# Where the final norm of the first 384 tokens is multiplied and stored: in one piece behind the last tokens' norm, or a tile per step of the last output products

## The chip, the cores and the metric

The kernel runs on one core of a Trainium2 chip. The metric is the device time of one execution in microseconds (us); lower is better. The engines are named as in the profile: PE (TensorE, with PEld for its weight loads), DVE (VectorE), ACT (ScalarE), POOL (GpSimd) and SP (SyncE, which here only issues DMAs).

## The reference

One inference step of a two-layer backbone (a Mamba-2 mixer, then differential attention, each followed by a gated convolutional feed-forward part), for 128 context tokens and 512 latent tokens of width 1024. Only its end matters here: the second layer's feed-forward part, its gated residual, and the final norm.

```python
def _rms(x):
    xf = x.astype(F32)
    return xf * lax.rsqrt(jnp.mean(xf * xf, axis=-1, keepdims=True) + EPS)

def rmsnorm(x, g):
    return (_rms(x) * g.astype(F32)).astype(x.dtype)
...
        xp = xp + p_g2 * conv_ffn(modulate(xp, norm_ffn_g[i], p_sh2, p_sc2), *ffn_p)
        xs = xs + s_g2 * conv_ffn(modulate(xs, norm_ffn_g[i], s_sh2, s_sc2), *ffn_p)
    y_prompt = rmsnorm(xp, final_norm_g)
    y_sample = rmsnorm(xs, final_norm_g)
```

## The kernel before

All activations are kept transposed: the width of 1024 lies in eight tiles of 128 partitions (`KT = 8`), and the 640 tokens lie along the free dimension. The residual stream is `self.x[0..7]`, which the profile calls `xr`. Matrix products are done three times in halves of a split float32 number (`mh`/`ml` and `whi`/`wlo`), so each step over one block of 128 inputs is three matmuls per part of the tokens.

The last feed-forward part ends in `project_last`, which makes the eight output tiles `po` of the down projection. For the first five tiles all 640 tokens are done at once. The last three tiles are done by parts of the tokens: first part C (tokens 0 to 383) of the three tiles, then part D (tokens 384 to 639) of the three. After each tile and part, `gate_add` on DVE adds the gated product to `xr` (L224; two instructions of 128 tokens for part D, since 128 of its tokens are latent and 128 context), and `norm_sq` squares the result on ACT (`nsq`, `sq`).

When a part's three tiles are written, its final norm is put in the list of tasks (`final_task`). A task is a generator; `hook()` is called after every step over one block of inputs (eight steps for each of the last tiles) and runs every task whose wait is over. `yield n` means: go on n steps later. `final_task` first makes the statistics: 32 small matmuls sum the squares into `ms`, nine small DVE instructions make the reciprocal root `rs_y`, and eight small matmuls spread it over the partitions into the PSUM tile `nbc`. Then, for each of the eight tiles, one DVE instruction makes `yt` = `xr` x gain x `nbc`, and a DMA stores it to `yT`: from the SP queue, for part D every second one from the ACT queue. The slots of `yt` come from a ring of 19 (`NF`) that other tiles also use.

Part C's task runs its statistics beside part D's products. Then it meets `yield 99`, which is more than the steps that are left, so its multiplications and stores come when the leftover tasks are drained, and these are drained in reverse order: part D's first, part C's behind it:

```python
            for t in reversed(list(self.tasks)):
                self.drain(t)
```

The order in which the engines receive the instructions is settled when the program is built; each engine then works through its own list in that order. `self.stt` is the DVE instruction of L224, and `self.mm` the matmul of L230.

Of the kernel before, what the change touches and what calls it, by code (L numbers as in the profile page):

```python
# [167 lines left out]
class Step:  # L168
# [1159 lines left out]
    def final_task(self, half):  # L1328

        bc = yield from self.norm_stats(half)  # L1330
        c0, c1 = HALF[half]
        if half == "C":
            yield 99
        for i in range(KT):
            t = self.slot("f", f"yt{i}", bufs=NF)
            self.stt(t[:, c0:c1], self.x[i][:, c0:c1], self.gains[:, 4 * KT + i:4 * KT + i + 1], bc[:, :c1 - c0],
                     ALU.mult, ALU.mult)
            eng = self.nc.scalar if half == "D" and i % 2 else self.nc.sync
            eng.dma_start(self.a["yT"][i, :, c0:c1], t[:, c0:c1])
# [211 lines left out]
```

## Time and profile before

| | |
|---|---|
| median of 3 runs | 1862.02 us (1861.01 to 1862.44) |
| profiled execution, its own time | 1865.19 us |
| span of the profiled execution, first to last instruction | 1863.4 us |
| PE busy | 1830.9 us, 98% of the span |
| DVE busy | 1464.3 us, 79% |
| ACT busy | 998.1 us, 54% |
| last matmul of part D's products starts | 1846.44 us |
| last multiplication of part C starts | 1859.46 us |
| last store is issued | 1860.10 us |

Times inside the profile count from the start of the span. A row of the timeline gives start, duration, engine, source line, operation, the tile written and those read, and shapes; in brackets stands how long the engine was idle before it and what ended that. The whole change lies in the last 25 us of the span.

### The profile page before, as it was taken

How to read it: one execution, taken by the hardware profiler on the slowest of the kernel's cores; microseconds unless marked ns; L12 is line 12 of the kernel's file. 1: busy time of each engine (PE TensorE's matmuls, PEld its weight loads, DVE VectorE, ACT ScalarE, POOL GpSimd, SP SyncE). 2: the span in 40 equal slices, each digit the busy share in tenths (PEclk: the TensorE clock that was granted, in tenths of full speed). 3: DMA queues.
4: the chain of work that ended last, by engine and by line, in shares of the span. 5: the costliest groups of instructions: out<-in, count | busy, mean ns of one | idle time of the engine just before them, and what ended most of it. 6: DMA issues, size and time to landing. Idle time of an engine off the chain costs nothing.

```text
span 1863.4 us, 33068 instructions
## 1 busy us (share of the span) xinstructions
PE 1830.9 (98%) x13057; PEld 1715.6 (92%) x13057; DVE 1464.3 (79%) x2827; ACT 998.1 (54%) x1862; POOL 55.7 (3%) x84
## 2 busy tenths in 40 slices
PE   7999999999999999999999999999999999999997
PEld 5899999999989999999999988888899999999996
DVE  5689999999848999998586877778779874874874
ACT  3379686879426442244363566566546543643641
POOL 0000000000001100011000000000001011100000
PEclk9999999999999999999999999999999999999998
DMA  9734244445547976677642211111047368853421
GB/s 339 270 108 147 92 126 128 114 132 177 184 148 220 279 217 211 208 205 201 208 133 77 88 46 59 57 52 49 21 129 193 95 180 237 250 166 103 142 80 57
DMA packets 108675, 276.06 MB, mean 148 GB/s; under 512 B 12284, under 2 KB 19048, under 8 KB 102504
## 3 DMA queue, kind: packets, MB, share of 16 engines
q1 hardware_dynamic: 100520, 225.19, 37.4%
q0 software_dynamic: 7424, 48.24, 11.0%
q8 instruction: 102, 1.67, 0.4%
q10 hardware_dynamic: 576, 0.52, 0.1%
q14 instruction: 53, 0.43, 0.1%
HBM read 267.95 MB, written 54.19 MB: 173 GB/s over the span
## 4 chain that ended last, share of the span: by engine, by line
PE 93%; DVE 3%; ACT 2%; DMA 1%; issue 1%; SPq 0%; DVEq 0%; ACTq 0%
PE po L230 25%; PE up L230 14%; PE bb L230 6%; PE ba L230 6%; PE bc L230 6%; PE z L230 6%; PE x L230 5%; PE st L230 5%; PE v L230 3%; PE yp L230 3%; PE q L230 2%; PE sl L230 2%; PE k L230 2%; PE ov L230 2%; PE in L230 1%; PE wt L1275 1%
## 5 line engine op out<-in xcount | busy, mean ns | idle before, releaser
L221 ACT ACTIVATE whi<-raw 128x1024 fp32r<-128x1024 f32 (+4 forms) x266 | 270.9, 1020 | 318.8 <-PE po L230 189.9
L227 DVE TENSOR_TENSOR wlo<-raw,whi 128x1024 fp32r<-128x1024 f32 (+4 forms) x266 | 312.4, 1175 | 79.8 <-ACT whi L221 68.2
L224 DVE SCALAR_TENSOR_TENSOR xr<-po,mod,xr 128x256 f32<-128x256 f32 (+2 forms) x231 | 89.0, 433 | 123.6 <-PE po L230 123.5
L230 PE MATMUL po<-ml,whi 128*128 128x256 f32 (+1 forms) x704 | 168.1, 310 | 0.0
L230 PE MATMUL po<-mh,whi 128*128 128x256 f32 (+1 forms) x704 | 167.8, 310 | 0.0
L230 PE MATMUL po<-mh,wlo 128*128 128x256 f32 (+1 forms) x704 | 167.8, 309 | 0.0
L230 PEld LDWEIGHTS po<-mh,whi 128*128 128x128 f32 x704 | 128.1, 188 | 0.8 <-ACT mh L221 0.5
L230 PEld LDWEIGHTS po<-mh,wlo 128*128 128x128 f32 x704 | 128.7, 188 | 0.0
L230 PEld LDWEIGHTS po<-ml,whi 128*128 128x128 f32 x704 | 128.5, 188 | 0.1
L230 PE MATMUL up<-h01h,wlo 128*128 128x256 f32 x464 | 105.7, 308 | 0.0
L230 PE MATMUL up<-h01l,whi 128*128 128x256 f32 x464 | 105.6, 308 | 0.0
L230 PE MATMUL up<-h01h,whi 128*128 128x256 f32 x464 | 105.6, 308 | 0.0
L230 PEld LDWEIGHTS up<-h01h,whi 128*128 128x128 f32 x464 | 84.4, 188 | 0.0
L230 PEld LDWEIGHTS up<-h01h,wlo 128*128 128x128 f32 x464 | 84.4, 188 | 0.0
L230 PEld LDWEIGHTS up<-h01l,whi 128*128 128x128 f32 x464 | 84.3, 188 | 0.0
L221 ACT ACTIVATE mh<-cv 128x640 fp32r<-128x640 f32 x44 | 32.4, 737 | 88.3 <-DVE cv L227 88.3
L221 ACT ACTIVATE e<-sl,sm 128x640 f32<-128x640 f32 x64 | 50.4, 790 | 40.2 <-DVE sm L1212 39.8
L688 DVE CUSTOM_DVE_ANT_0 junk<-mw,cbc 128x1024 bf16<-128x1024 f32 x48 | 58.5, 1219 | 8.4 <-DMA mw<-in_modT 8.3
L230 PE MATMUL z<-h00h,whi 128*128 128x256 f32 (+1 forms) x256 | 62.9, 325 | 0.0
L221 ACT ACTIVATE ca<-ca 128x640 f32<-128x640 f32 x44 | 32.3, 735 | 55.4 <-DVE ca L224 55.3
L230 PE MATMUL bb<-T,whi 128*128 128x320 f32 x264 | 61.6, 313 | 0.0
L221 ACT ACTIVATE e<-rb,Ctok 128x128 f32<-128x128 f32 x160 | 56.3, 389 | 8.5 <-issue 6.1
(580 smaller groups left out, 5317.5 us busy)
## 6 DMA issues: line engine op xcount, KB each, us to landing
wsum<-in_w_blk POOLq DMA_DIRECT2D x42, 768.0 KB, 7.1
raw<-in_w_blk SPq DMA_DIRECT2D x55, 512.0 KB, 4.0
mw<-in_modT SPq DMA_DIRECT2D x48, 512.0 KB, 4.4
raw<-wsum SPq DMA_DIRECT2D x92, 256.0 KB, 3.0
raw<-in_w_in SPq DMA_DIRECT2D x40, 512.0 KB, 5.4
rb<-rowd SPq DMA_DIRECT2D x40, 512.0 KB, 5.6
raw<-in_w_dn SPq DMA_DIRECT2D x32, 448.0 KB, 3.4
raw<-in_w_qkv SPq DMA_DIRECT2D x24, 512.0 KB, 3.3
```

The lines of the kernel that those rows point to most:

```text
L221: return self.pin(self.nc.scalar.activation(out, in_, func, **k))
L224: return self.pin(self.nc.vector.scalar_tensor_tensor(out, in0, s, in1, op0, op1))
L227: return self.pin(self.nc.vector.tensor_tensor(out, a, b, op))
L230: return self.pin(self.nc.tensor.matmul(out, lhsT, rhs, start=start, stop=stop, **k))
L688: nc.vector.tensor_tensor_reduce(w if c else junk, w, cb[:, c, :], 1.0, 0.0, ALU.mult, ALU.add, self.mod[l][:, t, c:c + 1])
L1275: nc.tensor.transpose(pm[:, b * P:(b + 1) * P], ws[b][:, kc * P:(kc + 1) * P], self.ident)
```

## The change

Part C's task no longer waits 99 steps ahead of its loop. It waits one step ahead of each of its eight tiles, so that a multiplication and a store are handed out with each of eight steps of part D's products. The instructions themselves stay the same, in number, shape and engine.

```diff
         bc = yield from self.norm_stats(half)
         c0, c1 = HALF[half]
-        if half == "C":
-            yield 99
         for i in range(KT):
+            if half == "C":
+                yield 1
             t = self.slot("f", f"yt{i}", bufs=NF)
```

On DVE, at the place where part D's residual additions stand (`xr_5203` and `xr_5205` are the residual tiles 6 and 7; those of 128 columns belong to part D), this is the piece of the difference:

```order
 L224 SCALAR_TENSOR_TENSOR rs_y<-rs_a,rs_y 128x96
+L224 SCALAR_TENSOR_TENSOR yt_20232<-xr_5191,gains,nbc 128x384
+L224 SCALAR_TENSOR_TENSOR yt_20238<-xr_5193,gains,nbc 128x384
+L224 SCALAR_TENSOR_TENSOR yt_20247<-xr_5195,gains,nbc 128x384
+L224 SCALAR_TENSOR_TENSOR yt_20253<-xr_5197,gains,nbc 128x384
+L224 SCALAR_TENSOR_TENSOR yt_20259<-xr_5199,gains,nbc 128x384
+L224 SCALAR_TENSOR_TENSOR yt_20265<-xr_5201,gains,nbc 128x384
+L224 SCALAR_TENSOR_TENSOR yt_20271<-xr_5203,gains,nbc 128x384
+L224 SCALAR_TENSOR_TENSOR yt_20277<-xr_5205,gains,nbc 128x384
 L224 SCALAR_TENSOR_TENSOR xr_5203<-po,mod_104,xr_5203 128x128 x2
 L224 SCALAR_TENSOR_TENSOR xr_5205<-po,mod_104,xr_5205 128x128 x2
```

The eight multiplications of part C now stand in one block behind part C's `rs_y` and ahead of part D's last four residual additions; before, they were the last eight instructions of DVE.

At the end of DVE's list stand part D's eight multiplications. In the kernel after the change they carry these waits (a name with `DMAHW` is the arrival of a DMA of the SP or ACT queue, here of a store that read the slot before):

```order
L224 SCALAR_TENSOR_TENSOR yt_20350<-xr_5191,gains,nbc 128x256 [waits DMAHW4_49,PE_49]
L224 SCALAR_TENSOR_TENSOR yt_20353<-xr_5193,gains,nbc 128x256 [waits DMAHW5_49]
L224 SCALAR_TENSOR_TENSOR yt_20356<-xr_5195,gains,nbc 128x256 [waits DMAHW6_49]
L224 SCALAR_TENSOR_TENSOR yt_20359<-xr_5197,gains,nbc 128x256 [waits DMAHW7_49]
L224 SCALAR_TENSOR_TENSOR yt_20362<-xr_5199,gains,nbc 128x256 [waits Activation_49]
L224 SCALAR_TENSOR_TENSOR yt_20365<-xr_5201,gains,nbc 128x256 [waits DMAHW0_49]
L224 SCALAR_TENSOR_TENSOR yt_20368<-xr_5203,gains,nbc 128x256 [waits DMAHW1_49]
L224 SCALAR_TENSOR_TENSOR yt_20371<-xr_5205,gains,nbc 128x256 [waits Activation_49]
```

Before, the first of these eight waited only for PE (`nbc`) and the other seven for nothing; now six of them are also told to wait for a store of part C, whose slot they take over.

SP's list before ended with four stores of part D (128x256) and the eight of part C (128x384), the last of them in this order:

```order
L1339 DMA out_yT<-yt_20338 128x256
L1339 DMA out_yT<-yt_20344 128x256
L1339 DMA out_yT<-yt_20350 128x384
L1339 DMA out_yT<-yt_20353 128x384
L1339 DMA out_yT<-yt_20356 128x384
L1339 DMA out_yT<-yt_20359 128x384
```

Now the eight of part C come first, and SP ends with four stores of part D:

```order
L1339 DMA out_yT<-yt_20265 128x384
L1339 DMA out_yT<-yt_20271 128x384
L1339 DMA out_yT<-yt_20277 128x384
L1339 DMA out_yT<-yt_20350 128x256
L1339 DMA out_yT<-yt_20356 128x256
L1339 DMA out_yT<-yt_20362 128x256
L1339 DMA out_yT<-yt_20368 128x256
```

ACT's list keeps its four stores of part D at its end. The lists of PE and POOL are the same as before.

## Prediction

> **What bounds the kernel now.** I read the page's summary first, then the chain of work that ended last in its final 20 us, then DVE's timeline there, and then the stores.
>
> ```profile
> span 1863.4 us, 33068 instructions
> ...
> PE 93%; DVE 3%; ACT 2%; DMA 1%; issue 1%; SPq 0%; DVEq 0%; ACTq 0%
> ```
>
> PE carries 93% of the chain, and the change leaves PE's list alone. So only the end, where PE no longer carries the chain, can move:
>
> ```profile
> 1845.90 0.84 PE po L230 x7
> ...
> 1847.40 0.42 ACT sq L221
> ...
> 1847.87 0.36 PE ms L230 x8
> ...
> 1850.67 1.95 PE nbc L230 x8
> ...
> 1857.44 2.62 DVE yt L224 x5
> ```
>
> Columns: start, duration, what. Behind the last product (the matmul rows end at 1846.73) the chain runs through part D's residual addition, square, sum, reciprocal root, the spreading matmuls, and then DVE's `yt` multiplications up to 1860.06. There are sixteen of these, D's eight and then C's eight. C's eight need only part C's `nbc`, which had been ready much earlier (below). They sit on the end path because of their place in DVE's list.
>
> ```profile
> 1836.22 0.62 DVE L224 SCALAR_TENSOR_TENSOR xr<-po,mod,xr 128x384 f32<-128x384 f32 x1 [3.62 <-PE po L230]
> ...
> 1843.93 0.61 DVE L224 SCALAR_TENSOR_TENSOR xr<-po,mod,xr 128x128 f32<-128x128 f32 x2 [2.92 <-PE po L230]
> 1846.76 0.61 DVE L224 SCALAR_TENSOR_TENSOR xr<-po,mod,xr 128x128 f32<-128x128 f32 x2 [2.21 <-PE po L230]
> ...
> 1852.64 7.42 DVE L224 SCALAR_TENSOR_TENSOR yt<-xr,gains,nbc 128x256 f32<-128x256 f32 x16 [2.12 <-PE nbc L230]
> ```
>
> This is DVE alone. The numbers in brackets show the room that the block moves into: DVE idles 2.92 us before the additions of tile 6 and 2.21 us before those of tile 7, waiting for PE's products both times. That is 5.13 us of holes, but tile 6's pair stands between them, and DVE works through its list in order.
>
> **The change part by part.** *What leaves the end.* C's eight multiplications as a group (busy time, mean ns of one), and their pace in the timeline:
>
> ```profile
> L224 DVE SCALAR_TENSOR_TENSOR yt<-xr,gains,nbc 128x384 f32<-128x384 f32 x8 | 4.3, 608 | 0.0
> ```
>
> ```profile
> 1855.78 1.13 DVE L224 SCALAR_TENSOR_TENSOR yt<-xr,gains,nbc 128x384 f32<-128x384 f32 x2
> ...
> 1859.46 0.61 DVE L224 SCALAR_TENSOR_TENSOR yt<-xr,gains,nbc 128x384 f32<-128x384 f32 x1
> ```
>
> The eight of C start at 1855.78 (first) and 1859.46 (eighth): seven steps, 0.526 us each, the next one starting before the last has ended (a single one takes 608 ns). The stores behind them:
>
> ```profile
> 1855.90 0.34 ACTq L1339 DMA_DIRECT2D out_yT<-yt  x1
> ...
> 1860.10 0.33 SPq L1339 DMA_DIRECT2D out_yT<-yt  x1
> ```
>
> ```profile
> out_yT<-yt SPq DMA_DIRECT2D x8, 192.0 KB, 1.9
> out_yT<-yt SPq DMA_DIRECT2D x4, 128.0 KB, 1.8
> out_yT<-yt ACTq DMA_DIRECT2D x4, 128.0 KB, 1.8
> ```
>
> D's last store goes out at 1855.90 (ACT queue, 1.8 us to landing), C's last at 1860.10 (SP queue, 1.9). When C's are no longer behind D's, the last store is issued 4.20 us earlier and lands 0.1 sooner: 4.30 us. The data bear this out from the other side:
>
> ```profile
> 1856.30:1860.20 3.90, 0.00 (x0) 0.00 (x0) 3.77 (x8) 0.00 (x0) 0.00 (x0) 0.50 0.97 349
> ...
> 1861.60:1861.80 0.20, 0.00 (x0) 0.00 (x0) 0.00 (x0) 0.00 (x0) 0.00 (x0) 0.50 0.17 56
> ```
>
> The last two columns are the share of the DMA engines and GB/s. In the last row a share of 0.17 is left, so the data stop near 1861.65, and the span ends at 1863.4, so 1.75 us of ending follows, which I leave as it is. D's eight stores are 1.05 MB; at 349 GB/s they need 3.0 us, about their pace on DVE (C's first starts 1855.78 - 1852.64 = 3.1 us behind D's first), so the DMA engines keep up and do not set a later end of their own.
>
> *What the block costs where it goes.* It waits for C's `nbc`:
>
> ```profile
> 1841.07 1.13 PE L230 MATMUL nbc<-rs_y,cst 128*128 128x96 f32 x8
> ```
>
> ```profile
> 1841.02:1843.93 2.91, 2.91 (x26) 2.87 (x26) 0.00 (x0) 0.28 (x1) 0.00 (x0) 1.00 0.00 0
> 1844.54:1846.76 2.22, 2.22 (x27) 2.09 (x29) 0.01 (x2) 0.42 (x1) 0.00 (x0) 1.00 0.00 0
> ```
>
> ```profile
> L224 DVE SCALAR_TENSOR_TENSOR xr<-po,mod,xr 128x128 f32<-128x128 f32 x2 | 0.6, 346 | 2.9 <-PE po L230 2.9
> ```
>
> `nbc` is done at 1842.20, and DVE starts 0.03 later. Eight at 0.526 fill 1842.23 to 1846.44. All four D additions stand behind them. Tile 6's pair was ready at 1843.93 and is now 2.5 us late, which by itself costs nothing: its square joins a sum that also needs tile 7's. Tile 7's pair was ready at 1846.76. Four additions take three steps and one whole one: a pair of 0.61 us with one at 346 ns makes the step 0.264, so 3 x 0.264 + 0.35 = 1.14 and the last ends at 1847.58, against 1847.37 before. The delay of the chain is **0.21 us**. ACT's square of tile 6 then runs 1847.00 to 1847.42, ahead of the one of tile 7 at 1847.60, so ACT adds nothing; PE's sums of tile 6 take about 0.36 us and also end before those of tile 7 begin.
>
> The step of 0.526 was measured with PE and its PSUM traffic at rest. The nearest row beside running matmuls is the addition of the same shape (128x384, a PSUM operand) at 1836.22: 0.62 us against 0.608, so I keep the step. The bounds: no delay at all (a block 0.21 us shorter), or no overlap between neighbours, 8 x 0.608 = 4.86 plus two pairs of 0.61, which ends at 1848.31, a delay of 0.94. I take 0.21, since the overlap is seen in this very group.
>
> [...]
>
> *SP and the stores of C.* The eight stores move ahead of D's on SP. One occupies SP for 0.33 us against a multiplication every 0.526, so SP keeps up and its last C store goes out near 1846.6. In both holes the DMA share is 0.00, so they meet no other transfer; nothing on the path reads their data. D's first store is wanted at about 1853.4, 6.8 us later. The cover of this cost of nothing is that stretch.
>
> *The new waits.* Six of D's multiplications wait for a landed store of C, their slot's last reader. With 1.9 us to landing, C's last lands at 1848.5; D's first multiplication is due at 1852.85. The waits are over 4.3 us before they are reached: nothing. ACT's four stores keep their place.
>
> *Sum.* 4.20 + 0.1 - 0.21 = 4.1 us off the span: 1863.4 becomes 1859.3, and the profiled time 1865.19 becomes 1861.1. That execution was 3.2 us slower than the median of the runs, and the change is at its end, where nothing scales; so 1862.02 - 4.1 = **1857.9 us**, 0.22% less. About 0.2% (3.7 us) is what a measurement of this kernel tells from no change, so the forecast lies close to that line.
>
> **The rivals.** *The additions of D come later than forecast, and the gain falls under the line.* For it: all eight multiplications stand in one block, not one per step, and the chain's four additions queue behind; at the bound without overlap the gain is 4.3 - 0.94 = 3.4 us, 1858.6. Against it: the step seen, and the 0.62 beside matmuls. From a delay of 0.6 us (a step of 0.575) the result counts as no change; a little unluck in the median of the runs does the same.
>
> *Slower.* The block is so slow beside PE that the delay eats the gain: 4.3 us of delay need tile 7's additions to start at about 1850.9 instead of 1846.76, so eight multiplications in 8.1 us, about 1.0 us each. At 1.1 us the time would be 1862.7. [...]
>
> *PE's clock.* The spreading matmuls of D run at half the granted clock:
>
> ```profile
> 1849.50:1850.00 0.50, 0.00 (x0) 0.00 (x0) 0.45 (x2) 0.00 (x0) 0.00 (x0) 0.60 0.00 0
> 1850.00:1850.50 0.50, 0.00 (x0) 0.00 (x0) 0.43 (x3) 0.00 (x0) 0.00 (x0) 0.50 0.00 0
> ```
>
> ```profile
> 556.55 1.10 PE L230 MATMUL nbc<-rs_y,cst 128*128 128x64 f32 x8
> ```
>
> The clock falls at 1849.6 (0.60 is the mean of that half microsecond), 1.07 us before D's `nbc`, which takes 1.95; the same eight at full clock took 1.10 at 556.55. If in the runs of the changed kernel the clock held 3 us longer, 0.85 us more would go: 1857.1. Against it: the products end at the same time, and a later `nbc` is further from the fall. [...]
>
> **How the numbers follow.** Forecast, gain near 4.1: 0.62. Clock held: 0.07, also faster. Late additions or a gain just under the line: 0.27, no change. Slower: 0.04. So faster 0.69, same 0.27, slower 0.04. The range: the late end is 1858.6 plus 0.7 (half of the spread of the runs shown, 1861.01 to 1862.44, which a median can miss by), with 0.1 for the span's ending: 1859.4. The early end takes half of the clock case and the same 0.7 below the forecast's best, 1857.7 (no delay), so 1857.7 - 0.4 - 0.7 = 1856.6.
>
> **What would show it.** Right: `yt` 128x384 on DVE from 1842.2 to 1846.5 at steps of 0.53, and tile 6's and 7's additions directly behind, ending near 1847.6; C's stores landed by 1848.6; D's multiplications from about 1852.85, preceded by a wait for PE and not for a DMA; the last store an ACT one near 1856.1, and a span of 1859.3. Wrong: steps of the block over 0.575, idle time between D's multiplications with a DMA as releaser, a store of D that lands clearly later than 1.8 us, or an ending behind the last data that is longer than 1.75 us.

## The result, and the profile after

| | before | after |
|---|---|---|
| median of 11 runs each | 1863.31 us | 1858.05 us |
| lowest to highest | 1860.54 to 1867.23 | 1854.39 to 1861.7 |
| span of the profiled execution | 1863.4 us | 1855.9 us |
| granted clock of PE, mean | 0.994 | 0.997 |

The ratio of after to before is 0.9974, interval 0.9964 to 0.9985: 0.26% faster, some 4.8 us (2.8 to 6.7). The forecast was 1857.9 us and 4.1 us less. The two spans differ by more than the runs do, 7.5 us, so the pair of profiles has to be taken apart before it is read.

DVE's timeline of the changed kernel, in the same columns as before:

```profile
1833.90 0.62 DVE L224 SCALAR_TENSOR_TENSOR xr<-po,mod,xr 128x384 f32<-128x384 f32 x1 [3.62 <-PE po L230]
...
1839.93 4.29 DVE L224 SCALAR_TENSOR_TENSOR yt<-xr,gains,nbc 128x384 f32<-128x384 f32 x8 [1.22 <-PE nbc L230]
1844.13 1.12 DVE L224 SCALAR_TENSOR_TENSOR xr<-po,mod,xr 128x128 f32<-128x128 f32 x4
...
1849.77 3.22 DVE L224 SCALAR_TENSOR_TENSOR yt<-xr,gains,nbc 128x256 f32<-128x256 f32 x8 [1.36 <-PE nbc L230]
```

The block of C's eight multiplications stands where the holes were, and the four additions of D follow it without idle time. Sixteen multiplications at the end have become eight. D's first waits for PE (`nbc`), not for a store of C. The stores, and the chain of work at the end:

```profile
1840.57 12.39 SPq L1339 DMA_DIRECT2D out_yT<-yt  x12
...
1850.67 2.69 ACTq L1339 DMA_DIRECT2D out_yT<-yt  x4
```

```profile
1838.91 0.99 PE nbc L230 x8
1839.90 0.03 issue
1839.93 4.29 DVE yt L224 x8
1844.22 1.05 DVE xr L224 x4
1845.26 0.02 issue
1845.29 0.43 ACT sq L221
1845.71 0.04 issue
1845.76 0.36 PE ms L230 x8
...
1848.56 1.19 PE nbc L230 x8
```

New on the chain is C's block itself: where the chain passed from D's last product to the additions, it now passes from C's `nbc` through the block. That is the small delay forecast, seen as a path.

The first row of DVE's timeline, tile 7's residual addition for part C, started at 1836.22 before. At that point, ahead of anything the change touches, this execution is already 2.32 us ahead. I therefore measure from that row's start to the span's end, and call it the end stretch: 1863.4 - 1836.22 = 27.18 us before, 1855.9 - 1833.90 = 22.00 after. The 2.32 us come from an earlier stage. PE's granted clock is the third column from the end (before, then after):

```profile
1050.00:1100.00 50.00, 49.31 (x302) 43.36 (x301) 37.01 (x79) 30.81 (x65) 0.00 (x0) 0.93 0.26 83
```

```profile
1050.00:1100.00 50.00, 49.15 (x319) 42.43 (x318) 38.95 (x82) 32.66 (x69) 0.00 (x0) 1.00 0.27 84
```

Before, PE ran at half clock from 1074.8 to 1081.6, 6.8 us, which makes the mean of 0.93; after, at no time in these 50 us. DVE's first multiplication of a norm ahead of that stretch (near 1021) and behind it (near 1390), before and then after:

```profile
1021.47 1.26 DVE L224 SCALAR_TENSOR_TENSOR nt<-xr,gs,nbc 128x256 f32<-128x256 f32 x3 [0.48 <-PE nbc L230]
...
1389.37 1.26 DVE L224 SCALAR_TENSOR_TENSOR nt<-xr,gs,nbc 128x256 f32<-128x256 f32 x3 [1.20 <-PE nbc L230]
```

```profile
1021.81 1.26 DVE L224 SCALAR_TENSOR_TENSOR nt<-xr,gs,nbc 128x256 f32<-128x256 f32 x3 [0.48 <-PE nbc L230]
...
1387.01 1.26 DVE L224 SCALAR_TENSOR_TENSOR nt<-xr,gs,nbc 128x256 f32<-128x256 f32 x3 [1.20 <-PE nbc L230]
```

At 1021 the changed kernel is still 0.34 us behind; near 1390 it leads by 2.36 us, and the lead stays. Nothing of the change lies ahead of it: this is a difference between executions. The mean of 0.93 in these 50 us comes back in a second profile of the kernel before, and also in one experiment built on the changed kernel (the multiplications done twice).

Of the 5.18 us by which the end stretches differ, D's `nbc` makes 0.76 (1.95 us before, 1.19 here). What the change has to do with that, and what the other 4.4 us consist of, is for the experiments.

### The profile page after: what moved, and what is told of

It is laid out like the page before. It is cut to its first block, busy times and chain, and to the rows that moved or that the text cites. A ratio compares the mean times of both kernels' runs of the same rounds, so it can differ in the third digit from the quotient of the medians.

```text
span 1855.9 us, 33067 instructions
## 1 busy us (share of the span) xinstructions
PE 1826.0 (98%) x13057; PEld 1711.2 (92%) x13057; DVE 1464.8 (79%) x2827; ACT 998.2 (54%) x1862; POOL 55.7 (3%) x84
## 4 chain that ended last, share of the span: by engine, by line
PE 93%; DVE 3%; ACT 2%; DMA 1%; issue 1%; SPq 0%; DVEq 0%; ACTq 0%
PE po L230 25%; PE up L230 14%; PE bb L230 6%; PE ba L230 6%; PE bc L230 6%; PE z L230 6%; PE x L230 5%; PE st L230 5%; PE yp L230 3%; PE v L230 3%; PE q L230 2%; PE sl L230 2%; PE k L230 2%; PE ov L230 2%; PE in L230 1%; PE modrow L230 1%
## 5 line engine op out<-in xcount | busy, mean ns | idle before, releaser
L230 PE MATMUL z<-h00l,whi 128*128 128x256 f32 (+1 forms) x256 | 59.8, 312 | 0.0
```

The costliest lines, as they stand in the source:

```text
L230: return self.pin(self.nc.tensor.matmul(out, lhsT, rhs, start=start, stop=stop, **k))
```

## The experiments

The theory is that of the prediction: C's multiplications and the data of its stores stood behind D's only by their place in the lists, and moved into idle time they cost nothing but 0.21 us. The rivals differ with each experiment. All were timed against the kernel before; the end stretch is read from each kernel's profile. Spans are printed to 0.1 us, so the difference of two end stretches is good to about 0.1 us; rows of the timeline are finer.

| kernel | ratio to before, interval | end stretch | D's `nbc` |
|---|---|---|---|
| before | | 27.18 us | 1.95 us |
| after | 0.9974, 0.9964 to 0.9985 | 22.00 | 1.19 |
| stores held back | 1.0006, 0.9997 to 1.0015 | 27.49 | 1.95 |
| multiplications twice | 1.0003, 0.9994 to 1.0012 | 26.01 | 1.96 |
| C drained first | 0.9978, 0.9969 to 0.9988 | 22.62 | 1.95 |
| C left out | 0.9986, 0.9978 to 0.9995 | 22.57 | 1.96 |
| after, PE kept busy | 0.9969, 0.9961 to 0.9978 | 21.89 | 1.09 |
| C first, PE kept busy | 0.9976, 0.9966 to 0.9986 | 21.71 | 1.09 |
| after again | 0.9975, 0.9966 to 0.9984 | 22.75 | 1.95 |
| before again | 0.9999, 0.9991 to 1.0008 | 27.25 | 1.96 |

**The stores held back.** Half of the change: the multiplications of C stay moved, their stores go back behind D's (a tag of its own for C's `yt`, so that no slot is shared, and all stores held in program order).

```diff
+            if half == "C":
+                self.held.append((self.a["yT"][i, :, c0:c1], t[:, c0:c1]))
+                continue
             eng = self.nc.scalar if half == "D" and i % 2 else self.nc.sync
...
             for t in reversed(list(self.tasks)):
                 self.drain(t)
+            for out, t in self.held:
+                self.tc.keep_in_program_order(self.nc.sync.dma_start(out, t))
```

> Part C's multiplications stay beside part D's products as in the changed kernel, its eight stores go back behind D's on SP. Measure: the end stretch, from the start of tile 7's residual addition for part C to the span's end (before 27.2 us, after 22.0). My theory, both the multiplications and the data of the stores had to leave the end: D's and C's data then queue, 1.05 MB at 340 and 1.57 MB at 365 GB/s, 7.4 us from D's first data, 4.2 us later than after, so the stretch is 26.2 us and the time within 0.1% of before. Rival, only DVE's multiplications count and stores are hidden: 22.0 us, 0.26% faster than before. Second rival, only the issue of eight more stores on SP counts (8 x 0.33 behind D's last): 24.3 us.

The whole gain is gone. The stores, and DMA share and GB/s in the last two columns:

```profile
1852.35 2.68 SPq L1342 DMA_DIRECT2D out_yT<-yt  x4
1855.09 3.99 SPq L1457 DMA_DIRECT2D out_yT<-yt  x8
```

```profile
1856.00:1860.00 4.00, 0.00 (x0) 0.00 (x0) 0.00 (x0) 0.00 (x0) 0.00 (x0) 0.50 1.01 366
...
1860.60:1860.90 0.30, 0.00 (x0) 0.00 (x0) 0.00 (x0) 0.00 (x0) 0.00 (x0) 0.50 0.24 82
```

DVE is done at 1855.1 and the DMA engines then run full at 366 GB/s to about 1860.67. From the stretch's start that is 25.46 us, against 20.40 in the changed kernel; less 0.76 for `nbc`, the data stop 4.30 us later, where 4.2 was expected. Both rivals fall. The eight stores do not go out every 0.33 us either, the time that one store of the kernel before holds SP, but every 0.50: the eight issues take 3.99 us, and the last starts near 1858.6 (1855.09 + 3.99 - 0.50). Why is not shown; the profile names nothing that SP waits for there. But 192 KB every 0.50 us would be 393 GB/s, more than the 366 that flow, so the data and not the issues set this end. So the end before had two limits of nearly the same length, DVE's sixteen multiplications and the data of sixteen stores, and moving the multiplications alone gives nothing. The stretch is 0.5 us over the expected 26.2 plus 0.76; 0.43 of it is a longer ending behind the data (2.03 us against 1.6).

**The multiplications twice.**

```diff
-            self.stt(t[:, c0:c1], ...
+            for _ in range(2 if half == "C" else 1):
+                self.stt(t[:, c0:c1], ...
```

> Each of part C's eight multiplications is done twice into the same tile. My theory, DVE's idle time beside part D's products is used up and what goes beyond it is paid one for one: 16 x 0.526 + four additions (1.06) + the reciprocal root (2.27) from C's nbc on, 3.2 us more than the changed kernel, end stretch 25.2 us. Rival, DVE has room enough there or the chain doesn't pass through it: 22.0 us.

```profile
1845.79 1.05 DVE yt L224 x2
1846.83 0.26 DVE xr L224
1847.09 1.05 DVE yt L224 x2
1848.14 0.14 DVE rs_v L307
1848.27 1.05 DVE yt L224 x2
1849.32 0.10 DVE rs_y L308
1849.43 1.07 DVE yt L224 x2
```

This is the chain: it no longer leaves DVE, and the surplus multiplications stand between the small instructions of D's reciprocal root. The stretch is 26.01, or 25.25 with `nbc` at 1.19; 25.2 was expected. In rows, D's last store is issued 23.08 us into the stretch, against 19.88 in the second profile of the changed kernel (below), where D's `nbc` is as long: 3.20 us more, as expected. What does not fit the idle time is paid one for one. The runs stand level with the kernel before; the 1.2 us that the stretch is shorter would be a ratio of 0.9994, the edge of their interval.

**C drained first.** The 99 steps stay, only the order at the end is turned.

```diff
-            for t in reversed(list(self.tasks)):
+            for t in list(self.tasks):
                 self.drain(t)
```

> The wait of 99 steps is kept, and only the order in which the leftover tasks are drained is turned: part C ahead of part D. In the list the multiplications then stand as three, tile 6's pair, four, tile 7's pair, one. My theory, the place in DVE's list is all that counts: each group fits its hole, tile 7's additions are not late, end stretch 0.2 us under the changed kernel, 21.8 us. Rival, handing one out per step matters, or the place behind the wait: 27 us, as before.

```profile
1841.70 1.66 DVE L224 SCALAR_TENSOR_TENSOR yt<-xr,gains,nbc 128x384 f32<-128x384 f32 x3 [1.22 <-PE nbc L230]
1843.40 0.61 DVE L224 SCALAR_TENSOR_TENSOR xr<-po,mod,xr 128x128 f32<-128x128 f32 x2
1843.92 2.18 DVE L224 SCALAR_TENSOR_TENSOR yt<-xr,gains,nbc 128x384 f32<-128x384 f32 x4
1846.22 0.61 DVE L224 SCALAR_TENSOR_TENSOR xr<-po,mod,xr 128x128 f32<-128x128 f32 x2
1846.74 0.61 DVE L224 SCALAR_TENSOR_TENSOR yt<-xr,gains,nbc 128x384 f32<-128x384 f32 x1
1847.72 0.23 DVE L307 TENSOR_SCALAR rs_v<-ms 128x64 f32<-128x64 f32 x1 [0.37 <-PE ms L230]
```

Each group fits its hole, and DVE still idles 0.37 us before `rs_v`. The stretch is 22.62 with `nbc` at 1.95, that is 21.86 at 1.19 (21.8 expected), and 0.13 under the changed kernel's second execution at the same clock. In rows, D's last store is issued 19.69 us into the stretch, 0.19 ahead of that execution, where 0.2 was expected. The long wait was not the cost; the place in the list was.

**C left out.** No multiplication and no store of part C, so 384 of 640 columns of the output stay unwritten.

```diff
+        if half == "C":
+            return
         for i in range(KT):
```

> Part C's multiplications and stores are left out (384 of 640 columns of the output are not written). My theory, in the changed kernel they cost 0.21 us of delay and nothing else: end stretch 21.8 us. Rival, the waits of D's multiplications for C's stores, the DMA traffic or the ending of the program still cost something: 21.5 us or less.

22.57 with `nbc` at 1.96, or 21.80. That equals C drained first within what the spans resolve, and in rows D's last store is issued 19.69 us into the stretch in both: in its best place the work of C costs nothing, and in the changed kernel 0.19 us (19.88 - 19.69). Waits for C's stores, their traffic and the ending add nothing that these rows show. The ratio, 0.9986, shows less gain than the profile's 4.6 us (which would be 0.9975). Single runs of one kernel spread by 6 us, so the end stretch is the finer measure; what made this kernel's runs slower elsewhere was not followed up.

**The changed kernel with PE kept busy.**

```diff
-        v, a = tile_("rs_v"), tile_("rs_a")
+        self.rv = v, a = tile_("rs_v"), tile_("rs_a")
...
+    def warm(self, t0):
+        if t0 == HALF["D"][0]:
+            wp = self.dense_ps("warm")
+            for _ in range(4):
+                self.mm(wp[:64, :256], self.rv[0], self.x[0][:, :256], True, True)
...
-        yield wait
+        yield self.warm(t0) or wait
```

> The changed kernel, with four added matmuls (64 x 256, their result unused) that can start once DVE has the first instruction of part D's reciprocal root, to keep PE busy until D's nbc. My theory, the 0.76 us beyond the forecast in the profile of the changed kernel came from where PE's clock fell in that execution and not from the change: with the clock held, D's eight nbc matmuls take 1.1 us here in any execution, end stretch 21.9 us. Rival, the clock falls all the same, or the added matmuls delay nbc: 1.95 us for nbc and 22.8 us or more.

```profile
1846.43 1.94 PE L230 MATMUL warm<-xr,rs_v 128*64 128x256 f32 x8 [0.35 <-DVE rs_v L307]
1848.56 1.08 PE L230 MATMUL nbc<-rs_y,cst 128*128 128x64 f32 x8 [0.19 <-DVE rs_y L224]
```

```profile
1848.50:1849.60 1.10, 1.04 (x8) 0.97 (x8) 0.00 (x0) 0.00 (x0) 0.00 (x0) 1.00 0.00 0
```

The four matmuls (eight rows) end before `rs_y` is there, the clock stays at 1.00, and `nbc` takes 1.09 us. The stretch is 21.89, as expected. The runs, at 0.9969, cannot tell it from the changed kernel: the intervals overlap.

**C drained first and PE kept busy.** The edits of both.

> The order of the third experiment (part C drained first at the end) together with the four matmuls that keep PE busy. If both readings hold, their gains add: D's nbc 1.1 us, tile 7's additions not late, end stretch 21.7 us, 0.8 us under the third experiment's 22.6 and the shortest so far; against before about 5.4 us, ratio 0.9971. Rival, they get in each other's way: 22.6 us.

21.71: the gains add, and this is the shortest end of all, 1.04 us under the changed kernel's second execution. By the ratio, 0.9976, the runs cannot tell it from the changed kernel.

**Both kernels again, unchanged.**

> The changed kernel once more, unchanged. If the clock's fall is a matter of the single execution, D's nbc takes 1.95 us in most executions (as in all four experiments so far) and the end stretch is 22.8 us; if the change itself holds the clock, it is 1.2 us and 22.0 us again, as in the first profile.

> The kernel before once more, unchanged, for a second look at its end stretch: 27.2 us with D's nbc at 1.95 us, or down to 26.3 us where the clock falls later. A time ratio within 0.1% of 1.

The changed kernel (first fence) and the kernel before (second), D's `nbc`:

```profile
1848.40 1.94 PE L230 MATMUL nbc<-rs_y,cst 128*128 128x64 f32 x8 [2.48 <-DVE rs_y L224]
```

```profile
1851.20 1.94 PE L230 MATMUL nbc<-rs_y,cst 128*128 128x64 f32 x8 [2.48 <-DVE rs_y L224]
```

This time the changed kernel pays the half clock in full: 22.75. So the 1.19 us of its first profile belonged to that execution. At equal clock the end stretches are 27.18 and 27.25 before and 22.75 after: the change is worth 4.4 to 4.5 us.

## Why the prediction was right

**The place and the sign.** PE's list and its work to the end of D's products were untouched, and the gain lies whole in the end stretch. The second executions give it to 0.1 us, and turning the drain order gives it without any wait taken away.

**The time itself was in part luck.** The forecast of 1857.9 us started from a median of three runs, 1862.02; over eleven runs the kernel before took 1863.31, 1.29 us more. The medians then differ by 5.26 us, 1.2 more than the forecast 4.1, and the two offsets nearly cancel in 1858.05. The comparison that counts is that of the gain: 4.1 us forecast, 4.4 to 4.5 in the end stretches, 2.8 to 6.7 in the runs.

**What leaves the end: 4.20 us.** The issue of the last store moved from 23.88 us (1860.10 - 1836.22) to 19.12 (1850.67 + 2.69 - 0.34 = 1853.02, less 1833.90) after the stretch's start, 4.76; less 0.76 for `nbc` that is 4.00, which is 4.20 less the delay of 0.2.

**The delay: 0.21 us.** The fourth addition of D ended 11.15 us into the stretch before (1847.37) and 11.35 after (1845.25): 0.20. The block took 4.29 us for the forecast 7 x 0.526 + 0.61 = 4.29: the step of 0.526 us taken with PE at rest held beside its matmuls.

**The covers.** Waits of D's multiplications for C's stores: none was reached, as the bracket behind D's first one shows (1.36 us, ended by PE's `nbc`) and as leaving C out confirms. SP and the DMA engines: free in that stretch, where the kernel before issues nothing on SP from 1836 to 1853.15, and where C's eight stores, 1.57 MB, are all that the DMA engines of the changed kernel move from 1839 to 1849. The prediction said that the DMA engines set no later end of their own, which is right for D alone; it did not say how near the data came to being the limit before. Holding the stores back showed it.

**The mis-sized term: landing, 0.1 us.** From the issue of the last store to the span's end it took 3.30 us before (1863.4 - 1860.10) and 2.88 after (1855.9 - 1853.02): 0.42 rather than 0.1. The forecast used the median time to landing of each group; no view gives the landing of the last store itself, which in the kernel before had others of C in front of it at a full DMA (0.97 of the engines), and the ending behind the data was taken as fixed. The end of the data after:

```profile
1854.20:1854.40 0.20, 0.00 (x0) 0.00 (x0) 0.00 (x0) 0.00 (x0) 0.00 (x0) 0.50 0.50 164
```

The data stop at 1854.30, 1.28 us after the last issue (before 1.55), and the ending takes 1.6 us (before 1.75). In the kernels that end in D's ACT store, the last issue lies 2.87 to 2.93 us ahead of the span's end; in those that end in a 192 KB store of C, 3.30, 3.36 and, held back, about 4.1. That the full queue in front makes the difference fits these numbers; no run separates it from the size of the store, and why the ending behind the data varies stays open. So the sum reads 4.20 - 0.20 + 0.42 = 4.42 us at equal clock.

**The rival of the clock** had a chance of 0.07. That the changed kernel holds the clock as a rule is refuted by its second profile; as something that happens in single executions it is real, and it made the first pair of profiles look 0.76 us better than the change is. Of the eight profiles with PE left alone, seven have `nbc` at 1.95 or 1.96. That is too few to say whether it happens more often in one kernel than in the other.

**A rival's sum.** For the rival "slower", a delay of 4.3 us puts tile 7's additions at 1851.06 and needs 1.04 us for each multiplication, and at 1.1 us each the time would be 1862.5, not 1862.7. Nothing hung on it; the step stayed at that of the forecast, 0.526 us.

**The line of 0.2%.** The forecast put 0.22% just above it; 0.26% was measured, with an interval from 0.15% to 0.36% that reaches across.

## What to carry to other kernels

Work that was ready long ago and only stands behind the last chain in an engine's list can be moved into that engine's idle time; price it as the overrun of the idle holes, instruction by instruction, and look who is queued behind. Ask too what is the limit right behind it: here multiplications and store data were equally long, and moving one without the other gained nothing. When a change at one place is worth 0.2%, compare stretches between fixed rows of the traces: here 2.3 us of the difference between the whole spans arose ahead of anything the change touches, where one execution ran for 6.8 us at half clock.

## What the runs showed of the hardware

In the eight profiles with PE left alone, its clock fell 2.8 to 5.0 us after the end of the last products (before: 1849.6 against 1846.73; the first profile of the changed kernel: 1849.4 against 1844.41), with the same instructions on PE up to there. The small matmuls of the sums follow the products; from the end of the last of them to the fall it was 1.2 to 3.3 us. So the place moves from execution to execution: 3.3 us behind the sums in the first profile of the changed kernel, 1.5 in its second. What sets it, and how little work makes the clock fall, no run here shows.

Eight small matmuls cost 1.95 us at half clock instead of 1.09. In both profiles with four matmuls put into PE's idle time ahead of them the clock held at 1.00 until 1853.7 and 1851.1, behind `nbc`, which is worth 0.86 us; the times of the runs are too coarse to show it.
